# Down products of a two-layer MLP in seven block multiplications, with the activations' sums made where the up product stores its result

## The chip, the core and the metric

The kernel runs on one core of a Trainium2 chip. The core has a matrix engine (TensorE; in the profile PE for its matmuls and PEld for its weight loads), a vector engine (VectorE, DVE), a scalar engine (ScalarE, ACT), a general engine (GpSimd, POOL), and queues that start transfers between DRAM and the on-chip memory SBUF (all of this part's transfers are issued by SyncE, SP). Matmul results land in PSUM, which has eight banks of 2 KB per partition. The metric is the device time of one execution, in microseconds.

## The reference, cut to what matters

```python
def sq_relu_mlp(h, norm_w, w_up, w_down):
    return h + jnp.square(jax.nn.relu(rmsnorm(h, norm_w) @ w_up)) @ w_down
...
for layer in range(DEPTH):                 # DEPTH = 2
    if layer < N_A_LAYERS:                 # layer 0: Mamba-2 mixer
        ...
        hm = sq_relu_mlp(hm, mlp_norm_w[layer], w_up[layer], w_down[layer])
    else:                                  # layer 1: sliding-window attention
        ...
    hp = sq_relu_mlp(hp, mlp_norm_w[layer], w_up[layer], w_down[layer])
    hs = sq_relu_mlp(hs, mlp_norm_w[layer], w_up[layer], w_down[layer])
```

The model width is 1024, the MLP's inner width 4096. Layer 0 has 1104 tokens (1024 of the prompt, 64 of the samples, 16 meta tokens), layer 1 has 1088 (no meta tokens). All is fp32.

## The kernel before, in words

Activations lie with features on the 128 partitions and tokens along the free axis. The stream `h` has 8 feature tiles, the MLP's inner activations have 32, which the kernel takes as 16 pairs f = 0 to 15. Tokens go in three chunks of 384, 384 and 336 (layer 1: 320). An fp32 product is made of three reduced-precision ones (`mm3`, L174 to L179): weights and activations are both split into a high part `hi` and a remainder `lo`, and hi·hi, hi·lo and lo·hi are added up in PSUM. So every operand needs a copy to `hi` on ScalarE and a subtraction for `lo`: for weights on GpSimd (`wunit` L162 and L163, `wparts` L853 and L854), for stored activations on VectorE (`block_parts`, L950 and L951).

**Up product.** Pairs 0 and 1 are made by plain multiplication (`plain_up`), the other fourteen by `up_pair`, each as a 2 by 2 block product in seven multiplications in place of eight (a Strassen-like scheme). Its sums of stream blocks are made once, ahead, by `sides`, over pairs of token quarters (`PAIRS`); its sums of weight blocks are made per pair on VectorE (`up_weights`, L863 and L869), and its seven products go to four pairs of PSUM banks `ma` to `md` in the order of `CHAIN` (L757): a, d, c, b, a, c, d. A pair takes 7 x 24 = 168 matmuls of 276 columns (layer 1: 272). VectorE and ScalarE combine the products into the tile `r` (named `rx` in the profile; there is one such buffer), square the positive part, and three transfers (L918 to L920) store it to DRAM, in `rd[f]`. The first write of the next pair into `r` is ScalarE's copy of product 1 (L900).

**Down product.** Eight blocks b of two pairs each, `down_block`: the block's activations are loaded from `rd` (`block_load`, L945) while the block before is multiplied, and split (`block_parts`). A block has four weight units of 256 output columns, each two output tiles times three chunks times 12 matmuls, so 4 x 2 x 3 x 12 = 288 matmuls. Each PSUM result is added to the stream `hh` in SBUF by VectorE (L724). The last block goes with the norm that follows it (layer 0) or with the final norm (layer 1).

**What sets the order.** The program is written in one order, and a scheduler of the framework, which simulates the engines' times, lays each engine's instructions out anew; each engine and each queue then runs its list strictly in order. Tiles with `bufs=1` or 2 make a writer wait for the last reader of the buffer. In layer 1, `second_layer` writes the first plain pair, the sides of the first pair of quarters, the norm of token chunk 1, and the sides of the second pair of quarters in this order, because the quarters 0 and 3 of the first `PAIRS` entry need only the chunks 0 and 2.

The functions that the change touches, with the profile's line numbers:

Of the kernel before, what the change touches and what calls it, by code (L numbers as in the profile page):

```python
# [8 lines left out]
F32 = mybir.dt.float32  # L9
F32R = mybir.dt.float32r  # L10
# [6 lines left out]
P = 128  # L17
# [23 lines left out]
PAIRS = [(0, 3), (1, 2)]  # L41
# [98 lines left out]
class Kernel:  # L140
# [735 lines left out]
    def up_pair(self, layer, f, rd):  # L876
# [45 lines left out]
    def up(self, layer, rd, R0):  # L922

        with ExitStack() as cq:
# [4 lines left out]
            for f in range(2, 16):  # L929
                self.up_pair(layer, f, rd)  # L930
# [22 lines left out]
    def down_block(self, layer, rd, b, bufs, hts, chs, tail=0, done=None):  # L953

        if b < 7:
            self.block_load(rd, b + 1, bufs[b + 1])
        x = {c: tuple(bufs[b][:, e, :, o:o + n] for e in range(2)) for c, (o, n) in enumerate(chs)}
        self.down(self.i["w_down"][layer, b], 4, x, hts, chs, tail, done,
                  step=(lambda u: self.block_parts(u, bufs[b + 1])) if b < 7 else None)
# [481 lines left out]
    def halves(self, n):  # L1441

        return [self.S[:, e].rearrange("p (a b) n -> p a b n", a=2)[:, :, :, :n] for e in range(2)]

    def first_layer(self, cb):
        nc = self.nc
        rd = [self.dram.tile([P, 2, T], F32, name="r_d%d" % f) for f in range(16)]
        h_d = self.dram.tile([P, KT, T], F32, name="h_d")
        with ExitStack() as ch:
# [27 lines left out]
            with ExitStack() as ct:  # L1477
# [28 lines left out]

    def second_layer(self, nx, cb):
        nc = self.nc
        chs = [(0, 384), (384, 384), (768, 320)]
        rd = [self.dram.tile([P, 2, META], F32, name="r_e%d" % f) for f in range(16)]  # L1510
        h_d = self.dram.tile([P, KT, META], F32, name="h_e")
        qw = META // 4
        with ExitStack() as cx:
# [22 lines left out]
            with ExitStack() as ce:  # L1536
# [7 lines left out]
                for i in (1, 2, 3):  # L1544
                    step(i, 0)
# [3 lines left out]
                for i in (1, 2, 3):  # L1549
                    step(i, 1)  # L1550
# [8 lines left out]
            self.up(1, rd, R0)  # L1559
            cr.close()  # L1560
            self.banks(self.ctx, 3)
            self.more_banks(self.ctx, 4)
            big = self.pool("h2", right=True).tile([P, KT, META], F32, name="hh")
            hts = [big[:, :, o:o + n] for o, n in chs]
            self.load_stream(big, h_d)
            bufs = [R0] + self.halves(META) * 4
            self.down_block(1, rd, 0, bufs, hts, chs)
        self.acc = {}
        self.fpool = self.pool("fin")
        for b in range(1, 8):  # L1570
            self.down_block(1, rd, b, bufs, hts, chs, 2 if b == 7 else 0,
                            (lambda c, u: self.final(c, u, hts, chs)) if b == 7 else None)
# [53 lines left out]
def _lay(a):  # L1626
# [18 lines left out]
        "w_down": a["w_down"].reshape(2, 8, 4, P, 4, 256).transpose(0, 1, 4, 3, 2, 5),  # L1645
        "w_kv": a["w_kv"].reshape(KT, P, 4, P).transpose(2, 1, 0, 3),
# [42 lines left out]
```

## Time and profile before

| | before |
|---|---|
| median of 3 runs | 3054.63 us (3051.82 to 3058.26) |
| the profiled execution | 3061.61 us, span 3059.9 us |
| granted TensorE clock, mean | 0.982 |
| TensorE, matmuls | 2935.1 us busy (96%), 19174 matmuls |
| TensorE, weight loads | 2804.4 us (92%) |
| VectorE | 1723.2 us (56%) |
| ScalarE | 1368.0 us (45%) |
| GpSimd | 1234.6 us (40%) |
| DMA | 305.84 MB, mean 100 GB/s |

All times that the next sections quote are from the one profiled execution, which took 7.0 us more than the median. Line numbers with an L are those of the kernel before, if nothing else is said. A busy share is an average over stages with different limits: the two up products (layer 0 from about 1155 to 1456 us, layer 1 from about 2360 to 2657 us) and the two down products that follow them are the stages that the change touches, and they are read by themselves.

### The profile page before, as it was taken

To read this page: it belongs to the slowest core of one execution; us is meant where nothing else is said; L and a number is where in the kernel's file an instruction comes from. 1 tells how busy PE (TensorE), PEld (TensorE's weight loads), DVE (VectorE), ACT (ScalarE), POOL (GpSimd) and SP (SyncE) were. 2 spreads that over 40 slices of the span, in tenths; PEclk is the share of its full clock that TensorE was granted. 3 is DMA by queue.
4 is the path that set the end of the run, shared out by engine and by line. 5 is a ranking of instruction groups with operands and counts; after the bars stand their busy time and mean duration, and the time that the engine had idled before them with its cause. 6 is when DMAs were issued, how large, how long until landed. Compare 5 with 4: busy or idle time off the path is not lost.

```text
span 3059.9 us, 48866 instructions
## 1 busy us (share of the span) xinstructions
PE 2935.1 (96%) x19174; PEld 2804.4 (92%) x19174; DVE 1723.2 (56%) x2964; ACT 1368.0 (45%) x2578; POOL 1234.6 (40%) x1055
## 2 busy tenths in 40 slices
PE   6999999989999989999999999998988999999998
PEld 4988888878999989999999998887878999999998
DVE  5777777865565575333433356776788433333335
ACT  5455555545444555444211126555655445412113
POOL 4456666654233214444211235464642444312122
PEclk8999999999999999999999999998999999999999
DMA  3244444454122223333432212122223233512221
GB/s 123 75 116 114 118 123 116 118 139 143 57 71 76 83 74 121 110 115 120 178 108 72 71 42 67 60 90 87 93 98 110 97 104 114 198 55 101 105 71 66
DMA packets 189854, 305.84 MB, mean 100 GB/s; under 512 B 27624, under 2 KB 138088, under 8 KB 187560
## 3 DMA queue, kind: packets, MB, share of 16 engines
q1 hardware_dynamic: 189624, 302.72, 31.3%
q8 instruction: 150, 2.46, 0.3%
q14 instruction: 80, 0.66, 0.1%
HBM read 232.72 MB, written 70.92 MB: 99 GB/s over the span
## 4 chain that ended last, share of the span: by engine, by line
PE 52%; DVE 7%; ACT 3%; issue 2%; POOL 1%; DMA 0%; DVEq 0%; POOLq 0%; ACTq 0%
PE g L177 10%; PE g L178 10%; PE g L179 10%; PE md L179 2%; PE mc L179 2%; PE md L178 2%; PE mc L177 2%; PE mc L178 2%; PE md L177 2%; PE ma L179 2%; PE ma L177 2%; PE ma L178 2%; PE mb L179 1%; POOL w L163 1%; PE mb L178 1%
## 5 line engine op out<-in xcount | busy, mean ns | idle before, releaser
L177 PE MATMUL g<-S,w 128*128 128x384 f32 (+2 forms) x2904 | 971.9, 335 | 17.5 <-DVE hh L724 4.8
L178 PE MATMUL g<-S,w 128*128 128x384 f32 (+2 forms) x2904 | 974.4, 336 | 2.8 <-DVE S L317 2.2
L179 PE MATMUL g<-S,w 128*128 128x384 f32 (+2 forms) x2904 | 968.2, 334 | 1.8 <-POOL w L163 1.8
L163 POOL TENSOR_TENSOR w<-raw,w 128x1024 fp32r<-128x1024 f32 x188 | 463.6, 2468 | 983.2 <-ACT w L162 924.1
L177 PEld LDWEIGHTS g<-S,w 128*128 128x128 f32 x2904 | 549.7, 189 | 26.3 <-issue 5.8
L178 PEld LDWEIGHTS g<-S,w 128*128 128x128 f32 x2904 | 550.2, 189 | 10.0 <-DVE S L317 3.2
L179 PEld LDWEIGHTS g<-S,w 128*128 128x128 f32 x2904 | 550.7, 190 | 8.2 <-issue 3.6
L724 DVE TENSOR_TENSOR hh<-hh,g 128x384 f32<-128x384 f32 (+2 forms) x552 | 288.3, 533 | 440.7 <-PE g L179 439.9
L162 ACT CAST w<-raw 128x1024 fp32r<-128x1024 f32 x188 | 197.2, 1049 | 611.8 <-PE g L178 561.8
L854 POOL TENSOR_TENSOR w<-s,w 128x512 fp32r<-128x512 f32 x112 | 150.4, 1346 | 252.3 <-ACT w L853 251.4
L532 DVE SCALAR_TENSOR_TENSOR fm<-xp,cv,fm 128x1024 f32<-128x1024 f32 x96 | 164.7, 1716 | 31.0 <-ACT fm L513 30.4
L854 POOL TENSOR_TENSOR w<-raw,w 128x512 fp32r<-128x512 f32 x84 | 113.4, 1351 | 90.6 <-ACT w L853 56.6
L179 PE MATMUL ma<-S,w 128*128 128x276 f32 (+1 forms) x448 | 129.5, 289 | 0.0
L177 PE MATMUL ma<-S,w 128*128 128x276 f32 (+1 forms) x448 | 129.5, 289 | 0.0
L177 PE MATMUL g<-gh,w 128*128 128x384 f32 (+1 forms) x384 | 126.9, 332 | 2.5 <-DVE hh L724 1.2
L178 PE MATMUL ma<-S,w 128*128 128x276 f32 (+1 forms) x448 | 129.1, 288 | 0.0
L178 PE MATMUL g<-gl,w 128*128 128x384 f32 (+1 forms) x384 | 126.5, 330 | 0.0
L179 PE MATMUL g<-gh,w 128*128 128x384 f32 (+1 forms) x384 | 126.1, 329 | 0.0
L585 ACT ACTIVATE dec<-ab,acs 128x128 f32<-128x128 f32 (+1 forms) x288 | 91.1, 389 | 68.1 <-PE y L594 63.8
L863 DVE TENSOR_TENSOR s<-raw 128x512 f32<-128x512 f32 x56 | 45.8, 834 | 110.5 <-DMA raw<-in_w_up_dram 82.7
L630 POOL TENSOR_TENSOR yt<-yt,yo 128x256 f32<-128x256 f32 (+1 forms) x72 | 68.4, 949 | 88.4 <-DVE yt L627 82.4
L1143 ACT ACTIVATE es<-es,few 128x273 f32<-128x273 f32 (+2 forms) x136 | 70.9, 526 | 55.3 <-DVE few L1141 41.4
(390 smaller groups left out, 6715.2 us busy)
## 6 DMA issues: line engine op xcount, KB each, us to landing
raw<-in_w_up_dram SPq DMA_DIRECT2D x64, 512.0 KB
raw<-in_w_down_dram SPq DMA_DIRECT2D x64, 512.0 KB
raw<-in_w_in_dram SPq DMA_DIRECT2D x48, 512.0 KB
ab<-acs_d SPq DMA_DIRECT2D x64, 256.0 KB
S<-r_e SPq DMA_DIRECT2D x28, 544.0 KB
S<-r_d SPq DMA_DIRECT2D x24, 552.0 KB
raw<-in_w_q_dram SPq DMA_DIRECT2D x24, 512.0 KB
raw<-in_w_o_dram SPq DMA_DIRECT2D x24, 512.0 KB
```

The source lines that it names most:

```text
L162: nc.scalar.copy(out=wh, in_=raw)
L163: nc.gpsimd.tensor_tensor(out=wl, in0=raw, in1=wh.bitcast(F32), op=ALU.subtract)
L177: mm(out=out, lhsT=wh, rhs=xh, start=(first and k == 0), stop=False)
L178: mm(out=out, lhsT=wh, rhs=xl, start=False, stop=False)
L179: mm(out=out, lhsT=wl, rhs=xh, start=False, stop=(k == n - 1))
L532: nc.vector.scalar_tensor_tensor(out=acc[:, :SEQ], in0=xp[:, k:k + SEQ], scalar=cv[:, j, k:k + 1], in1=acc[:, :SEQ], op0=ALU.mult, op1=ALU ...
L585: nc.scalar.activation(out=dec[:n, h, :n], in_=ab[:n, h, :n], func=AF.Relu, scale=-1.0, bias=self.acs[:n, t, 4 * g + h:4 * g + h + 1])
L630: nc.gpsimd.tensor_tensor(out=yt[:, :, :no], in0=yt[:, :, :no], in1=yo[:, :, :no], op=ALU.add)
L724: nc.vector.tensor_tensor(out=hv, in0=hv, in1=pt[:, :n], op=ALU.add)
L854: nc.gpsimd.tensor_tensor(out=t[:, 1], in0=src, in1=t[:, 0].bitcast(F32), op=ALU.subtract)
L863: add = lambda a, b, op: (lambda t: (nc.vector.tensor_tensor(out=t, in0=a, in1=b, op=op), t)[1])(self.wsum([P] + sh))
L1143: nc.scalar.activation(out=e, in_=e, func=AF.Exp, bias=m[:, h:h + 1], accum_out=den[:, h:h + 1])
```

## The change

The middle twelve pairs, f = 2 to 13, get their down product in seven block multiplications too. They form four blocks of three pairs (`KB = 3`). The 2 by 2 blocks are: the two feature tiles of a pair, the output tiles p and p + 4, and the two token halves; so `PAIRS` becomes (0, 2), (1, 3), by which the two quarter pairs of the up product fill token halves.

- **Up.** `up_pair` of these twelve pairs adds five VectorE operations: three of 552 columns (`m1`, a new `r[:, 1]`, `u`) and two of 276 (`o5`). Each has both inputs in SBUF. Seven right sides are stored, in `rt`, by five transfers (`m1`, `r` with its four blocks, `u`, two pieces of `o5`). Pairs 14 and 15 store `r` to `rd` in one transfer, with no sums.
- **Down.** Block 0 (pairs 0 and 1) stays plain, now with all eight PSUM banks as single ones. While it runs, the first seven right sides, 128 partitions x 1656 elements (848 KB) each, are loaded and split. Then `down_blocks` goes through four blocks b, in each through four groups p of two output tiles. A group is seven products of 2 token pieces x 3 pairs x 3 = 18 matmuls of 276 columns (272 in layer 1), so 126 matmuls, into `ma` to `md` in the order of `CHAIN`. Per group VectorE makes four sums of weight blocks (384 columns; the weights are laid out for it as `w_downs`) and seven evictions of 552 columns, into `hh` or into a temporary `us` (the very first group's first one is ScalarE's); in block b = 3 it adds `us` to three parts of `hh` per group. GpSimd makes seven remainders of 384 columns per group.
- **The right sides' buffers.** Each block's seven slots are taken from `S`, `R0` and two new tiles `A5`, `A6`. Most of a block's slots are free only when the last group of the block before, or the first of its own, is under way, so five to seven splits per block (one ScalarE copy and one VectorE subtraction of 1656 elements each) stand around the change of blocks.
- **The last block** (pairs 14 and 15, b = 7) stays plain, as before.
- **Layer 1.** Both quarter pairs now need chunk 1, so the sides' steps 1 to 3 of the first quarter pair move behind `stream.norm(1)`.

Matmuls: six plain blocks of 288 become four blocks of 504, per layer 1728 become 2016, of 276 columns in place of 384, 384 and 336.

```diff
-PAIRS = [(0, 3), (1, 2)]
+PAIRS = [(0, 2), (1, 3)]
+KB = 3
...
-        rv = r.rearrange("p (f i) n -> p f i n", i=2)
-        nc.sync.dma_start(out=rd[f][:, :, 0:n], in_=rv[:, :, 0])
-        nc.sync.dma_start(out=rd[f][:, :, 3 * qw:4 * qw], in_=rv[:, :, 1, 0:qw])
-        nc.sync.dma_start(out=rd[f][:, :, n:3 * qw], in_=rv[:, :, 1, qw:n])
+        if not 2 <= f < 14:
+            nc.sync.dma_start(out=rd[f].rearrange("p f (i n) -> p (f i) n", i=2), in_=r)
+            return
+        sub = lambda out, x, y: nc.vector.tensor_tensor(out=out, in0=x, in1=y, op=ALU.subtract)
+        d = rt[(f - 2) // KB][:, :, :, (f - 2) % KB]
+        sub(m1, r[:, 1], r[:, 0])
+        nc.sync.dma_start(out=d[:, 0, 1], in_=m1)
+        sub(r[:, 1], r[:, 3], r[:, 1])
+        nc.sync.dma_start(out=d[:, :, 0], in_=r)
+        sub(u, r[:, 3], m1)
+        nc.sync.dma_start(out=d[:, 1, 1], in_=u)
+        for k in range(2):
+            t = self.n1("o5")[:, :qw]
+            cs = slice(k * qw, k * qw + qw)
+            sub(t, r[:, 2, cs], u[:, cs])
+            nc.sync.dma_start(out=d[:, 2, 1, cs], in_=t)
...
+    def down_weights(self, layer, b, p):
...
+        yield self.wparts(a11, sh)
+        s1 = add(a21, a22, ALU.add)
+        yield self.wparts(s1, sh)
+        d = add(a11, a21, ALU.subtract)
+        nc.vector.tensor_tensor(out=s1, in0=s1, in1=a11, op=ALU.subtract)
+        yield self.wparts(d, sh)
+        yield self.wparts(s1, sh)
+        yield self.wparts(a12, sh)
+        yield self.wparts(a22, sh)
+        yield self.wparts(add(a12, s1, ALU.subtract), sh)
...
+    def down_blocks(self, layer, rd, rt, R0, big, c0, chs):
...
+        slots = [A, B + A[:5], A[5:] + B + A[:3], A[3:] + A[:3]]
+        free = [(0, 1, 2, 3, 4), (0, 1, 2, 3, 4), (0, 1, 4, 5, 6), ()]
+        def load(b, i):
+            nc.sync.dma_start(out=slots[b][i][:, 1].bitcast(F32), in_=rt[b][:, i // 2, i % 2])
+        def parts(b, i):
+            x = slots[b][i]
+            nc.scalar.copy(out=x[:, 0], in_=x[:, 1].bitcast(F32))
+            nc.vector.tensor_tensor(out=x[:, 1], in0=x[:, 1].bitcast(F32), in1=x[:, 0].bitcast(F32), op=ALU.subtract)
...
+        def step(b, p, i):
+            if b == 3:
...
+            elif p == 0 and i == 0:
+                load(b + 1, 0)
+                load(b + 1, 1)
+            elif p in (1, 2) and i == 2:
+                parts(b + 1, p - 1)
+            elif p == 3 and i in free[b]:
+                load(b + 1, free[b].index(i) + 2)
+            if p == 3 and i > 4 and b < 3:
+                parts(b + 1, i - 3)
+            if p == 0 and i < 3 and b:
+                parts(b, 4 + i)
...
+        for b in range(4):
+            for p in range(4):
...
+                for i, (wh, wl) in enumerate(self.down_weights(layer, b, p)):
+                    e = self.CHAIN[i]
...
+                    x = slots[b][i]
+                    for k in range(2):
+                        cs = slice(k * qw, k * qw + qw)
+                        self.mm3(banks[e][:, 512 + (k - 1) * qw:512 + k * qw], [(wh[:, q], wl[:, q]) for q in range(KB)],
+                                 [(x[:, 0, q, cs], x[:, 1, q, cs]) for q in range(KB)], new)
+                    pv = banks[e][:, 512 - qw:512 + qw]
+                    to = (uv, hv[1][1], hv[1][1], uv, hv[0][0], hv[1][0], hv[0][1])[i]
+                    if i == 0 and b == 0:
+                        nc.scalar.copy(out=uv, in_=pv)
+                    else:
+                        tt(to, pv, to)
+                    if i == 3 and b == 3:
+                        for to in (hv[1][1], hv[1][0], hv[0][1]):
+                            tt(to, to, uv)
+                    step(b, p, i)
...
-                for i in (1, 2, 3):
-                    step(i, 0)
                 stream.norm(1)
                 for _ in plain:
                     pass
                 for i in (1, 2, 3):
-                    step(i, 1)
+                    for k in range(2):
+                        step(i, k)
```

The scheduler's lists show what moves. The first place is VectorE in the down product of layer 0. Before, inside a block (a block's activations are split while the one before is multiplied; `g` is a single PSUM bank):

```order
L724 TENSOR_TENSOR hh_14867<-hh_14867,g_15630 128x384
L951 TENSOR_TENSOR S_90<-S_90 128x1104
L724 TENSOR_TENSOR hh_14867<-hh_14867,g_15644 128x384
L951 TENSOR_TENSOR S_90<-S_90 128x1104 x2
L724 TENSOR_TENSOR hh_14867<-hh_14867,g_15658 128x336
L951 TENSOR_TENSOR S_90<-S_90 128x1104
L724 TENSOR_TENSOR hh_14867<-hh_14867,g_15672 128x384
```

Now, at the change from block b = 0 to b = 1 (L1056 is the eviction and L1024 the split, both lines of the kernel after; `md_15915` is the last product of the old block's last group, `ma_16067` the first of the new block):

```order
L1056 TENSOR_TENSOR hh_14966<-mc_15942,hh_14966 128x552
L1024 TENSOR_TENSOR S_90<-S_90 128x1656
L1056 TENSOR_TENSOR hh_14966<-md_15915,hh_14966 128x552
L1024 TENSOR_TENSOR S_90<-S_90 128x1656 x2
L1056 TENSOR_TENSOR us_14978<-ma_16067,us_14978 128x552
L1024 TENSOR_TENSOR A5_14979<-A5_14979 128x1656
L1056 TENSOR_TENSOR hh_14966<-md_16096,hh_14966 128x552
L1024 TENSOR_TENSOR A6_14980<-A6_14980 128x1656
L1056 TENSOR_TENSOR us_14978<-mb_16149,us_14978 128x552
L1056 TENSOR_TENSOR hh_14966<-mc_16124,hh_14966 128x552
```

Five splits, longer than before, now stand between the evictions that free the banks `md`, `ma` and `mc`, where before four stood in a block of 24 evictions. The second place is VectorE at the end of a pair in the up product of layer 0. Before (`n3_13166` is `u`, `s` are weight sums):

```order
L882 TENSOR_TENSOR rx_13040<-md_13080,n3_13166 128x552
L863 TENSOR_TENSOR s_13529<-raw_13497 128x512
L863 TENSOR_TENSOR s_13560<-raw_13495,raw_13497 128x512
L882 TENSOR_TENSOR rx_13269<-mc_13341,rx_13269 128x552
L869 TENSOR_TENSOR s_13529<-s_13529,raw_13495 128x512
```

Now (L885, L865 and L923 are lines of the kernel after):

```order
L885 TENSOR_TENSOR rx_13098<-md_13138,n3_13224 128x552
L865 TENSOR_TENSOR s_13605<-raw_13573 128x512
L923 TENSOR_TENSOR n3_13131<-rx_13098 128x552
L923 TENSOR_TENSOR rx_13098<-rx_13098 128x552
L923 TENSOR_TENSOR n3_13224<-rx_13098,n3_13131 128x552
L923 TENSOR_TENSOR o5_13326<-rx_13098,n3_13224 128x276
L923 TENSOR_TENSOR o5_13329<-rx_13098,n3_13224 128x276
L865 TENSOR_TENSOR s_13636<-raw_13571,raw_13573 128x512
L885 TENSOR_TENSOR rx_13336<-mc_13408,rx_13336 128x552
```

The five new operations stand between the last eviction of a pair and the first of the next that waits for the store of `r`, behind a weight sum that waits for its transfer. The order of TensorE's matmuls in the up product is the same as before.

More of the change, by code (lines that the diff above doesn't have):

```diff
@@ L929, in up @@
             for f in range(2, 16):
-                self.up_pair(layer, f, rd)
+                self.up_pair(layer, f, rd, rt)
                 if f == 8:
@@ L951, in block_parts, with down_block @@
         nc.vector.tensor_tensor(out=lo, in0=lo.bitcast(F32), in1=hi.bitcast(F32), op=ALU.subtract)
[L953 to L959, printed above, removed]
+    def down_block(self, layer, b, buf, hts, chs, tail=0, done=None, step=None):
+        x = {c: tuple(buf[:, e, :, o:o + n] for e in range(2)) for c, (o, n) in enumerate(chs)}
+        self.down(self.i["w_down"][layer, b], 4, x, hts, chs, tail, done, step=step)
@@ new lines, in down_weights, with add @@
+    def down_weights(self, layer, b, p):
+        nc = self.nc
+        sh = [KB, P]
+        raws = []
+        for j in range(2):
+            t = self.np.tile([P, 2, KB, P], F32, tag="n3", bufs=2, name="raw") if p % 2 else self.raw([P, 2, KB, P])
+            nc.sync.dma_start(out=t, in_=self.i["w_downs"][layer, b, p, :, j])
+            raws.append(t)
+        (a11, a12), (a21, a22) = ((t[:, 0], t[:, 1]) for t in raws)
+        def add(a, b, op):
+            t = self.np.tile([P] + sh, F32, tag="n1", bufs=5, name="s")
+            nc.vector.tensor_tensor(out=t, in0=a, in1=b, op=op)
+            return t
+        yield self.wparts(a11, sh)
[8 more added lines that the diff above has]
+        yield self.wparts(add(a12, s1, ALU.subtract), sh)
@@ L1447, in first_layer @@
         rd = [self.dram.tile([P, 2, T], F32, name="r_d%d" % f) for f in range(16)]
+        rt = [self.dram.tile([P, 4, 2, KB, T // 2], F32, name="t_d%d" % b) for b in range(4)]
         h_d = self.dram.tile([P, KT, T], F32, name="h_d")
@@ L1510, in second_layer @@
         rd = [self.dram.tile([P, 2, META], F32, name="r_e%d" % f) for f in range(16)]
+        rt = [self.dram.tile([P, 4, 2, KB, META // 2], F32, name="t_e%d" % b) for b in range(4)]
         h_d = self.dram.tile([P, KT, META], F32, name="h_e")
@@ L1558, in second_layer @@
             R0 = self.pool("R0", ctx=cx).tile([P, 2, 4, META], F32R, name="R0")
-            self.up(1, rd, R0)
+            self.up(1, rd, rt, R0)
             cr.close()
+            big = self.pool("h2", right=True).tile([P, KT, META], F32, name="hh")
+            self.load_stream(big, h_d)
+            with ExitStack() as c0:
+                self.down_blocks(1, rd, rt, R0, big, c0, chs)
             self.banks(self.ctx, 3)
             self.more_banks(self.ctx, 4)
-            big = self.pool("h2", right=True).tile([P, KT, META], F32, name="hh")
+            self.acc = {}
+            self.fpool = self.pool("fin", ctx=cx)
             hts = [big[:, :, o:o + n] for o, n in chs]
[L1565 to L1572, printed above, removed]
+            self.down_block(1, 7, R0, hts, chs, 2, lambda c, u: self.final(c, u, hts, chs))
     def mixer(self, c1):
```

57 lines of the change are left out of this document (46 added, 11 removed).

## The prediction, before the result was known

> **What bounds the kernel now.** I read the page's busy table first, then the table of stages for the four stages that the change touches:
>
> ```profile
> PE 2935.1 (96%) x19174; PEld 2804.4 (92%) x19174; DVE 1723.2 (56%) x2964; ACT 1368.0 (45%) x2578; POOL 1234.6 (40%) x1055
> ```
>
> ```profile
> core 0: us, PE busy (x) PEld busy (x) DVE busy (x) ACT busy (x) POOL busy (x), PEclk, DMA share, GB/s
> 1300.00:1350.00 50.00, 50.00 (x397) 50.00 (x396) 16.32 (x20) 26.10 (x43) 21.97 (x17) 1.00 0.32 104
> 1550.00:1600.00 50.00, 50.00 (x299) 50.00 (x299) 18.11 (x29) 9.75 (x9) 9.81 (x5) 1.00 0.28 97
> ...
> 2750.00:2800.00 50.00, 50.00 (x304) 50.00 (x303) 18.09 (x30) 8.63 (x8) 9.64 (x4) 1.00 0.25 88
> ```
>
> The first row lies in the up product of layer 0, the second and third in the down products of the two layers. In each PE is busy 50.00 us of 50 at the full granted clock and nothing else is near its limit. The view of PE's waits is empty from 1176.3 to 1442, from 1440 to 1800 and from 2400 to 2640 us. So a matmul saved there is time saved, until another engine falls behind.
>
> What a matmul costs, I take from the repeats of a stage in SyncE's list. Starts of one and the same transfer, one pair or one block apart (columns: start, duration):
>
> ```profile
> 1325.07 0.33 SPq L847 DMA_DIRECT2D raw<-in_w_up_dram  x1
> ...
> 1346.37 0.33 SPq L847 DMA_DIRECT2D raw<-in_w_up_dram  x1
> ...
> 1548.94 1.99 SPq L945 DMA_DIRECT2D S<-r_d  x4
> ...
> 1597.26 1.84 SPq L945 DMA_DIRECT2D S<-r_d  x4
> ```
>
> ```profile
> 2550.19 0.33 SPq L847 DMA_DIRECT2D raw<-in_w_up_dram  x1
> ...
> 2571.37 0.33 SPq L847 DMA_DIRECT2D raw<-in_w_up_dram  x1
> ...
> 2751.87 2.14 SPq L945 DMA_DIRECT2D S<-r_e  x4
> ...
> 2799.60 1.75 SPq L945 DMA_DIRECT2D S<-r_e  x4
> ```
>
> Layer 0: a pair takes 21.30 us for 168 matmuls, 126.8 ns each; a plain block 48.32 us for 288, 167.8 ns each. Layer 1: 21.18 us, 126.1 ns, and 47.73 us, 165.7 ns.
>
> **The change part by part.**
>
> *TensorE.* Six blocks go and 2016 matmuls come that have the up product's form: 276 (272) columns, fp32r, two pieces of a bank pair. Layer 0: 6 x 48.32 = 289.9 removed, 2016 x 126.8 ns = 255.6 added, -34.3. Layer 1: 286.4 removed, 254.2 added, -32.2. Together **-66.5 us**. This is the whole gain; the rest is what comes back.
>
> *VectorE and GpSimd in a group.* These rows price VectorE's operations with their partners:
>
> ```profile
> L882 DVE TENSOR_TENSOR rx<-rx,n x28: 726/1808/1822, 1175.2 to 2648.7; 128x552 f32<-128x552 f32 x14, 128x544 f32<-128x544 f32 x14
> L882 DVE TENSOR_TENSOR rx<-mc,n x28: 719/726/733, 1177.5 to 2654.0; 128x552 f32<-128x552 f32 x14, 128x544 f32<-128x544 f32 x14
> ...
> L951 DVE TENSOR_TENSOR S<-S x52: 1279/1294/1997, 1464.6 to 2952.2; 128x1088 fp32r<-128x1088 f32 x28, 128x1104 fp32r<-128x1104 f32 x24
> ```
>
> ```profile
> L863 DVE TENSOR_TENSOR s<-raw 128x512 f32<-128x512 f32 x24 | 19.2, 815 | 54.2 <-DMA raw<-in_w_up_dram 41.9 <-POOL w L854 12.4
> L882 DVE TENSOR_TENSOR rx<-rx,n 128x552 f32<-128x552 f32 x13 | 19.1, 1472 | 0.4
> L869 DVE TENSOR_TENSOR s<-s,raw 128x512 f32<-128x512 f32 x12 | 11.5, 961 | 14.3 <-POOL w L854 14.3
> ...
> L863 DVE TENSOR_TENSOR s<-raw,s 128x512 f32<-128x512 f32 x13 | 8.8, 681 | 0.0
> ...
> L854 POOL TENSOR_TENSOR w<-s,w x112: 1274/1292/2359, 1147.1 to 2640.1; 128x512 fp32r<-128x512 f32 x112
> ```
>
> (The forms with slashes are shortest, median, longest in ns over the whole run; those with bars are count, busy us and mean ns in the up product of layer 0.) A group of `down_blocks` is 126 x 126.8 ns = 15.98 us on PE. VectorE's seven evictions of 552 columns take 0.73 each (second row: one input from PSUM), its four weight sums 681 x 384/512 = 0.51 each, in all 7.2 us. GpSimd's remainders are 1292 x 384/512 = 0.97, seven make 6.8. An ordinary group is covered by PE twice over, and costs nothing.
>
> *The change of blocks.* A split of 1656 elements is 1294 x 1656/1096 = 1.96 us on VectorE, seven make 13.7, and most of them stand within two groups, the last of the old block and the first of the new. So these 31.9 us of PE carry 2 x 7.2 + 13.7 = 28.1 us of VectorE, at the last change (b = 2 to 3) 14.4 + 5 x 1.96 + four of block 7's splits at 1.29 + three `us` adds at 0.73 = 31.6. That is where cover runs out, for a reason that the first two rows show: the operation of 552 columns with both inputs in SBUF has a shortest time of 726 ns and a median of 1808, the one with an input from PSUM never passes 733. GpSimd's operations stretch likewise, from 1274 to 2359. The two engines get in each other's way when VectorE has two SBUF inputs, and a meeting costs VectorE some 1.08 us. Fifteen such operations stand at a change (seven splits, eight weight sums), with GpSimd busy 14 x 0.97 = 13.6 us of 31.9. None meeting: the lists are strictly in order, an eviction of `md` or `mc` waits behind a split or two, and PE loses perhaps 0.5 us. All meeting, at a mean overlap of three quarters of the 1.08: 15 x 0.81 = 12.2, so 28.1 + 12.2 = 40.3, 8.4 over. In the up product the 62 operations with two SBUF inputs stretch by 24 x 0.134 + 12 x 0.280 + 13 x 0.746 = 16.3 us over 681 (for 552 columns, 726), 0.26 each. I take this row mean: 15 x 0.26 = 3.9, so 32.0 against 31.9 at the first two changes and 35.5, 3.6 over, at the last. With an eviction's wait behind the splits I take 2.5, 2.5 and 4, **+9 per layer, +18** in all, with ends of +3 (6 x 0.5) and +50 (6 x 8.4).
>
> The Trainium skill ("SBUF — State Buffer", section "SBUF: two separate sides") says that VectorE and GpSimd share a port pair under an exclusive lock held for a whole instruction, so that a VectorE operation with two SBUF inputs and a GpSimd operation that reads SBUF block each other fully. The trace agrees (726 against 1808 ns). By that rule taken at its word, each of the fifteen operations would meet one, and the sum would use the upper end, +50 in place of +18.
>
> *The other parts of the down product.* The `us` adds of b = 3 (three a group, both inputs in SBUF) stand among evictions, +1 per layer, +2; ends 0 and +8. The first seven right sides are loaded during block 0, with the stream and the weights some 13.7 MB. The highest rate a row shows:
>
> ```profile
> 1448.00:1450.00 2.00, 2.00 (x18) 2.00 (x18) 0.00 (x0) 1.06 (x2) 1.75 (x1) 1.00 1.05 426
> ```
>
> At about 400 GB/s that is 34 of 48.3 us, hidden by block 0's matmuls; at half the rate it would be 20 us late per layer. I take +0.5 each, **+3 with the `us` adds**.
>
> *The up product's store.* Five VectorE operations (726 to 1808 ns) and two more transfers per pair; VectorE has the room (16.32 of 50 us). What matters is the loop through the single buffer `r`:
>
> ```profile
> 1333.96 0.62 ACT L900 COPY rx<-md 128x552 f32<-128x552 f32 x1 [0.80 <-DMA r_d<-rx]
> ...
> 1335.21 0.73 DVE L882 TENSOR_TENSOR rx<-mc,rx 128x552 f32<-128x552 f32 x1 [2.90 <-PE mc L179]
> ...
> ACT rx L900 <- DMA r_d<-rx: 27.8, 12, 6.1
> ```
>
> ```profile
> 1326.05 0.73 DVE L882 TENSOR_TENSOR rx<-md,n 128x552 f32<-128x552 f32 x1 [2.32 <-PE md L179]
> ...
> 1329.36 0.69 DVE L863 TENSOR_TENSOR s<-raw 128x512 f32<-128x512 f32 x1 [2.58 <-DMA raw<-in_w_up_dram]
> ```
>
> `md` of the last product is evicted at 1326.05; ScalarE's copy of product 1 into `r` goes at 1333.96, having waited 0.80 us for the store, in the early pairs up to 6.1 us. What it feeds is the eviction of `mc` at 1335.21, which must be done when PE's product 5 writes `mc`: five products of 3.04 us (21.30/7) after 1326.0, at 1341.2. From 1333.96 that leaves 1341.2 - 1333.96 - 0.62 - 0.73 - 0.15 (semaphores) = 5.7 us. After, `r` leaves only when the first two differences are made, behind a weight sum that itself waits for its transfer (1329.36), and with three quarters more bytes (seven blocks in place of four). I estimate its landing 2.7 to 4.3 us later than now (two differences of 0.73 to 1.81, the wait of up to 2.58, the longer transfer, less what they overlap), so 5.7 - 4.3 = 1.4 us or more is left in the steady pairs, and nothing in the first ones, where the wait is already 6.1. **+3 us** over both layers, ends 0 and +12.
>
> *Layer 1's start.* Around it PE waits:
>
> ```profile
> PE g L223 <- ACT msh L221: 6.7, 1, 6.7
> PE md L177 <- ACT w L853: 2.7, 1, 2.7
> ...
> 2299.92 1.27 DVE L795 TENSOR_TENSOR t<-X 128x1088 f32<-128x1088 f32 x1
> ...
> 2314.31 0.55 DVE L222 TENSOR_TENSOR msl<-acc,msh 128x384 fp32r<-128x384 f32 x1
> ```
>
> The 6.7 us are PE's wait for the norm of chunk 1, whose `msl` stands on VectorE behind the first quarter pair's sides (L795). The sides move behind it, so most of this wait goes; the sides then come late to the first pairs, which can lengthen the 2.7 us. **-2.5**, ends -6.7 and +3.
>
> Sum: -66.5 + 18 + 3 + 3 - 2.5 = -45.0. Against the profiled execution's 3061.6 that is 3016.6; this execution stood 7.0 above the median, so on the scale of the median **3009.6 us**.
>
> **The rivals.**
>
> *B, nothing comes back.* GpSimd and VectorE miss each other and the splits fit. For it: 28.1 of 31.9 us without a meeting, and the scheduler fills a wait for `md` with half a product into `mc`. Then -66.5 + 3 - 2.5, about **2989**.
>
> *C, VectorE and GpSimd lock each other at every change of blocks.* For it: the median of 1808, not 726, in the one operation whose place is fixed relative to GpSimd's. Against it: the splits' own median of 1294 beside its minimum of 1279, though GpSimd is less busy there (9.81 of 50 us). Then -66.5 + 50 + 3.5, **3042**.
>
> *D, slower: the store loop lengthens each pair.* The copy of product 1 waits for `r`, its dependent eviction frees `mc` late, and PE stands in each of the 24 changed pairs. It decides from a landing 5.7 + 1.9 = 7.6 us later than now: at 1.9 us a pair (45/24) no gain is left. At 3 us a pair it costs 72, **3082**. For it: the 6.1 us waits, and the larger store on five transfers; against it: the DMA share of 0.32 in this stage.
>
> *E, a wait at each group takes the gain.* The last product's `md` is needed again after one product of the next group, now 18 matmuls (2.3 us) in place of 24 (3.04 us in the up product, where the view of waits is empty). The eviction's 0.73 us and its semaphores fit, unless VectorE's list is behind. At 2 us in each of the 32 groups, 64 us, nothing is left: **3052**. This is also how the change could fail to do what it says.
>
> **How the numbers follow.** Forecast 0.58 (its own range 2990 to 3033), B 0.14, C 0.14, E 0.06, D 0.08. A measurement of this kernel can tell about 0.2%, 6 us, from no change. Faster by more: forecast, B and C, less a little of C's upper end: 0.85. Within: E and that little, 0.07. Slower: D, 0.08. The range takes in B below and C above with some of C's spread: 2983 to 3046.
>
> **What the changed profile would show.** Right: about 19,750 matmuls (19174 + 2 x 288); a pair still 21.3 us apart; the splits at a block's change between 1.96 and 3 us; PE's waits on evictions from VectorE there, 2 to 4 us per change, and hardly any elsewhere in the down product; the 6.7 us wait gone. Wrong: PE's waits between pairs of the up product, with `r`'s store as their end (D); waits in every group (E); block changes of over 8 us (C); or a spacing in `down_blocks` other than 126.8 ns, which would resize the main term.

## The result, and the profile after

| | before | after |
|---|---|---|
| median | 3054.24 us (4 runs, 3051.82 to 3058.26) | 3009.99 us (4 runs, 3003.57 to 3013.72) |
| ratio | | 0.9852 (95% interval 0.9828 to 0.9875) |
| the profiled execution | 3061.61 us, span 3059.9 | 3013.72 us, span 3012.0 |

The change made the kernel 44 us faster. The profiled execution of after is the slowest of its four, 3.7 us above their median. The busy row of its page:

```profile
PE 2876.1 (95%) x19750; PEld 2743.4 (91%) x19750; DVE 1963.2 (65%) x3172; ACT 1453.5 (48%) x2770; POOL 1397.4 (46%) x1231
```

There are 576 matmuls more and TensorE is busy 59 us less. To see where the time went I cut both profiles at matmuls that both programs have: the first into `ma` (start of the up product's pairs) and the first of blocks 0 and 7 into a single bank `g`. The views by tile give first and last starts (of all forms; `g<-R` are the blocks that read `R0`). Before, layer 0, block 0 and block 7:

```profile
L177 PE MATMUL g<-R,w x33: 312/334/342, 1453.6 to 1469.9; 128*128 128x384 f32 x24, 128*128 128x336 f32 x9
...
L177 PE MATMUL g<-R,w x96: 312/334/341, 1791.9 to 1839.8; 128*128 128x384 f32 x64, 128*128 128x336 f32 x32
```

After, the same two, and those of layer 1:

```profile
L179 PE MATMUL g<-R,w x96: 312/334/341, 1451.9 to 1499.8; 128*128 128x384 f32 x64, 128*128 128x336 f32 x32
L179 PE MATMUL g<-R,w x96: 312/334/411, 1770.4 to 1818.4; 128*128 128x384 f32 x64, 128*128 128x336 f32 x32
...
L179 PE MATMUL g<-R,w x96: 306/334/338, 2630.3 to 2677.3; 128*128 128x384 f32 x64, 128*128 128x320 f32 x32
...
L179 PE MATMUL g<-R,w x96: 303/334/422, 2943.9 to 2993.0; 128*128 128x384 f32 x64, 128*128 128x320 f32 x32
```

| stretch | before | after | difference | forecast |
|---|---|---|---|---|
| start to the first `ma`, layer 0 | 1155.2 | 1151.7 | -3.5 | 0 |
| up product, layer 0 | 298.4 | 300.2 | +1.8 | +3 with layer 1 |
| block 0 to block 7, layer 0 | 338.3 | 318.5 | -19.8 | -23.8 |
| block 7 to the first `ma`, layer 1 | 558.9 | 554.2 | -4.7 | -2.5 |
| up product, layer 1 | 307.0 | 305.7 | -1.3 | |
| block 0 to block 7, layer 1 | 334.1 | 313.6 | -20.5 | -21.7 |
| block 7 to the end | 68.0 | 68.1 | +0.1 | 0 |

(Before, the layer 1 blocks are taken as seven periods of 47.73 us.) Most of the gain, 40.3 of 47.9 us, lies in the two down products. Within them, the view of TensorE's waits from 1500 to 1770 us, empty before, now has four rows:

```profile
PE md L179 <- DVE hh L1056: 3.7, 2, 2.3
PE ma L179 <- DVE us L1056: 3.2, 2, 1.6
PE mc L179 <- DVE hh L1056: 1.3, 2, 0.6
PE mb L181 <- POOL w L856: 0.3, 1, 0.3
```

VectorE's timeline shows where they are. The change from b = 0 to b = 1 (columns: start, duration, what it is, and in brackets the idle time before it):

```profile
1538.30 0.73 DVE L1056 TENSOR_TENSOR hh<-md,hh 128x552 f32<-128x552 f32 x1 [4.98 <-PE md L181]
...
1554.31 0.73 DVE L1056 TENSOR_TENSOR hh<-md,hh 128x552 f32<-128x552 f32 x1 [4.98 <-PE md L181]
...
1567.82 2.06 DVE L1024 TENSOR_TENSOR S<-S 128x1656 fp32r<-128x1656 f32 x1
1569.80 0.72 DVE L1056 TENSOR_TENSOR hh<-md,hh 128x552 f32<-128x552 f32 x1
1570.44 4.68 DVE L1024 TENSOR_TENSOR S<-S 128x1656 fp32r<-128x1656 f32 x2
1575.04 0.72 DVE L1056 TENSOR_TENSOR us<-ma,us 128x552 f32<-128x552 f32 x1
1575.69 2.03 DVE L1024 TENSOR_TENSOR A<-A 128x1656 fp32r<-128x1656 f32 x1
1577.64 0.72 DVE L1056 TENSOR_TENSOR hh<-md,hh 128x552 f32<-128x552 f32 x1
...
1605.96 0.73 DVE L1056 TENSOR_TENSOR hh<-md,hh 128x552 f32<-128x552 f32 x1 [2.70 <-PE md L181]
```

In an ordinary group VectorE stands idle for 4.98 us before `md` comes, and groups follow each other in 16.0 us (1538.30 to 1554.31). Between 1562.3 and 1588.1 no row has a bracket: VectorE never waits, and evictions come one or two splits after their matmuls. The next `md` that VectorE waits for, at the same place in its group, comes 51.65 us and three groups later, 3.6 more than three groups take. In the same way the other changes cost 3.4 and 5.6 us in layer 0, and 2.1, 2.2 and 7.6 in layer 1.

At the last change of each layer a part of this is the clock, which the rows of waits don't show. Right after TensorE's longest wait there (2.30 us for `md` in layer 0, 2.69 in layer 1) the granted clock reads 0.50 for 3.41 us, and matmuls that start 127 ns apart elsewhere start 230 ns apart. Three stretches of equal length, the halved one of layer 0, one 10 us later, and the halved one of layer 1 (clock in the third column from the end, the first count in brackets is TensorE's matmuls):

```profile
1709.42:1712.83 3.41, 3.41 (x17) 3.41 (x17) 3.41 (x3) 0.00 (x0) 2.23 (x1) 0.50 0.00 0
1719.42:1722.83 3.41, 3.41 (x29) 3.41 (x29) 3.41 (x7) 0.85 (x2) 1.46 (x2) 1.00 0.08 10
2890.43:2893.84 3.41, 3.41 (x17) 3.41 (x16) 3.41 (x7) 0.51 (x1) 1.62 (x2) 0.50 0.00 0
```

I estimate this at 3.41 x (1 - 127/230) = 1.5 us of the 5.6 and of the 7.6.

The up product kept its pace, one pair in 21.33 us (SyncE's list):

```profile
1260.28 2.36 SPq L849 DMA_DIRECT2D raw<-in_w_up_dram  x2
...
1281.61 2.35 SPq L849 DMA_DIRECT2D raw<-in_w_up_dram  x2
```

### The profile page after: what moved, and what is told of

Read it like the earlier page. It is cut to its first block, busy times and chain, and to the rows that moved or that the text cites. A ratio compares the mean times of both kernels' runs of the same rounds, so it can differ in the third digit from the quotient of the medians.

```text
span 3012.0 us, 50781 instructions
## 1 busy us (share of the span) xinstructions
PE 2876.1 (95%) x19750; PEld 2743.4 (91%) x19750; DVE 1963.2 (65%) x3172; ACT 1453.5 (48%) x2770; POOL 1397.4 (46%) x1231
## 4 chain that ended last, share of the span: by engine, by line
PE 45%; DVE 9%; ACT 4%; issue 3%; POOL 2%; DMA 2%; SPq 0%; DVEq 0%; POOLq 0%; ACTq 0%
PE g L179 3%; PE g L180 3%; PE g L181 3%; PE mc L179 3%; PE mc L181 3%; PE mc L180 3%; PE md L181 3%; PE md L180 3%; PE md L179 3%; PE ma L179 3%; PE ma L181 3%; PE ma L180 3%; PE mb L179 1%; PE mb L180 1%; PE mb L181 1%
## 5 line engine op out<-in xcount | busy, mean ns | idle before, releaser
L179 PE MATMUL g<-S,w 128*128 128x384 f32 (+3 forms) x1656 | 561.3, 339 | 17.5 <-DVE hh L726 4.8
L180 PE MATMUL g<-S,w 128*128 128x384 f32 (+3 forms) x1656 | 562.8, 340 | 3.6 <-DVE S L319 3.0
L181 PE MATMUL g<-S,w 128*128 128x384 f32 (+3 forms) x1656 | 557.5, 337 | 1.8 <-POOL w L165 1.8
L856 POOL TENSOR_TENSOR w<-s,w 128x384 fp32r<-128x384 f32 (+1 forms) x240 | 326.5, 1363 | 367.0 <-ACT w L855 355.2
L856 POOL TENSOR_TENSOR w<-raw,w 128x384 fp32r<-128x384 f32 (+1 forms) x180 | 222.8, 1240 | 268.0 <-ACT w L855 251.9
L179 PEld LDWEIGHTS g<-S,w 128*128 128x128 f32 (+1 forms) x1656 | 315.1, 190 | 26.2 <-issue 5.9
L180 PEld LDWEIGHTS g<-S,w 128*128 128x128 f32 (+1 forms) x1656 | 315.1, 190 | 10.6 <-DVE S L319 4.1
L181 PEld LDWEIGHTS g<-S,w 128*128 128x128 f32 (+1 forms) x1656 | 315.2, 190 | 8.0 <-issue 3.3
L855 ACT CAST w<-s 128x384 fp32r<-128x384 f32 (+1 forms) x240 | 134.4, 562 | 211.3 <-PE ma L181 69.9
L179 PE MATMUL ma<-S,w 128*128 128x276 f32 (+1 forms) x736 | 212.9, 289 | 5.0 <-DVE us L1056 5.0
L180 PE MATMUL ma<-S,w 128*128 128x276 f32 (+1 forms) x736 | 212.5, 289 | 1.1 <-DVE S L820 0.9
L181 PE MATMUL ma<-S,w 128*128 128x276 f32 (+1 forms) x736 | 212.4, 289 | 0.0
L726 DVE TENSOR_TENSOR hh<-hh,g 128x384 f32<-128x384 f32 (+2 forms) x264 | 134.1, 530 | 68.8 <-PE g L181 68.3
L179 PE MATMUL md<-S,w 128*128 128x276 f32 (+1 forms) x464 | 135.5, 292 | 8.9 <-DVE hh L1056 8.7
L179 PEld LDWEIGHTS ma<-S,w 128*128 128x128 f32 x736 | 138.6, 188 | 5.7 <-ACT w L855 3.6
L180 PEld LDWEIGHTS ma<-S,w 128*128 128x128 f32 x736 | 138.7, 188 | 1.6 <-DVE S L820 1.1
L181 PEld LDWEIGHTS ma<-S,w 128*128 128x128 f32 x736 | 138.5, 188 | 0.0
L179 PE MATMUL mc<-S,w 128*128 128x276 f32 (+1 forms) x464 | 134.7, 290 | 3.9 <-DVE hh L1056 2.6
```

What stands on the lines that cost most here:

```text
L179: mm(out=out, lhsT=wh, rhs=xh, start=(first and k == 0), stop=False)
L180: mm(out=out, lhsT=wh, rhs=xl, start=False, stop=False)
L181: mm(out=out, lhsT=wl, rhs=xh, start=False, stop=(k == n - 1))
L726: nc.vector.tensor_tensor(out=hv, in0=hv, in1=pt[:, :n], op=ALU.add)
L855: nc.scalar.copy(out=t[:, 0], in_=src)
L856: nc.gpsimd.tensor_tensor(out=t[:, 1], in0=src, in1=t[:, 0].bitcast(F32), op=ALU.subtract)
```

## The experiments

**What costs at a change of blocks.** My theory was that VectorE's own work there, in its strict order and stretched by GpSimd, is longer than TensorE's. The rivals: the loads of the right sides come too late, or the length of the list alone counts. Four runs pull these apart.

*e1*, the VectorE half of the splits left out for b = 1 to 3 (the remainder slot keeps the unsplit value):

```diff
             nc.scalar.copy(out=x[:, 0], in_=x[:, 1].bitcast(F32))
-            nc.vector.tensor_tensor(out=x[:, 1], in0=x[:, 1].bitcast(F32), in1=x[:, 0].bitcast(F32), op=ALU.subtract)
+            if b == 0:
+                nc.vector.tensor_tensor(out=x[:, 1], in0=x[:, 1].bitcast(F32), in1=x[:, 0].bitcast(F32), op=ALU.subtract)
```

> Left out: VectorE's half of the split (x - hi) of the right sides of blocks b = 1 to 3 in both layers, 42 operations of 1.88 to 2.7 us; the remainder slot keeps the unsplit value. ScalarE's copy, all loads, evictions, sums and matmuls stay. My theory (at a change of blocks VectorE's strictly ordered list is longer than PE's work, so PE waits behind it): the changes, which now cost 3.6 + 3.4 + 5.6 us in layer 0 and about 2.2 + 2.3 + 5 in layer 1, lose nearly all of it: 3010 goes to about 2990. Rival (the loads of the right sides come too late, since their slots are freed late): the loads stay where they are, 3010 stays within 5 us.

Measured: 2986.26 us, ratio to before 0.9768 (0.9749 to 0.9788). In layer 0, block 7 starts 312.7 us after the up product's last matmul into `ma` (324.7 after: the changes' 12.6 us are gone), and the view of TensorE's waits has one row there:

```profile
PE md L179 <- DVE hh L1057: 0.3, 1, 0.3
```

All loads are still in place, so they are not what TensorE waits for.

*e2*, GpSimd's remainders of the weights left out in the down blocks (the matmuls take the high part twice):

```diff
-        yield self.wparts(a11, sh)
+        yield self.whigh(a11, sh)      # t[:, 0], t[:, 0]: no GpSimd operation
...
```

> Left out: GpSimd's remainders of the weights in the seven-product down blocks (7 per group, 224 in all); the matmuls that used them take the high part instead, so their count stays. My theory: VectorE's operations with two SBUF inputs no longer meet GpSimd, so at a change the seven splits fall from about 14.6 to 13.2 us and the weight sums from 8 to 4.3, 5 us less than PE's cover needs: the 12.6 us of layer 0's changes fall to about 3, in all 3010 to about 2994. Rival (the list's length alone counts, meetings don't): within 4 us of 3010.

Measured: 2993.19 us, ratio 0.9790 (0.9772 to 0.9807). All VectorE operations are still there, but they are shorter. The costliest groups of VectorE in layer 0's blocks, after (columns: count, busy us, mean ns, idle time before):

```profile
L1024 DVE TENSOR_TENSOR S<-S 128x1656 fp32r<-128x1656 f32 x13 | 27.2, 2108 | 2.0 <-ACT S L1023 2.0
L986 DVE TENSOR_TENSOR s<-raw 128x384 f32<-128x384 f32 x28 | 24.9, 928 | 0.0
```

and in e2:

```profile
L1029 DVE TENSOR_TENSOR S<-S 128x1656 fp32r<-128x1656 f32 x13 | 24.1, 1877 | 1.5 <-ACT S L1028 1.5
...
L991 DVE TENSOR_TENSOR s<-raw 128x384 f32<-128x384 f32 x28 | 14.3, 553 | 0.0
```

The same 28 weight sums take 24.9 us beside GpSimd and 14.3 without it. Without meetings the unchanged list fits under TensorE's time (one wait of 1.2 us is left). So the list's length alone doesn't make the loss.

*e5*, one VectorE operation more at each change (a split slot's maximum with itself):

```diff
                 parts(b, 4 + i)
+                if i == 1:
+                    x = slots[b][5][:, 1]
+                    nc.vector.tensor_tensor(out=x, in0=x.bitcast(F32), in1=x.bitcast(F32), op=ALU.max)
```

> The changed kernel with one more VectorE operation at each change of blocks (the maximum of a split slot with itself, 1656 elements, 128 partitions, some 1.9 to 2.3 us; the values stay). My theory (VectorE's time is the bound at a change): each extra microsecond there is a microsecond of the whole, six times 1.9 to 2.3: 3010 becomes 3021 to 3024. Rival (PE waits there for something else, and VectorE has slack): within 4 us of 3010.

Measured: 3026.42 us, ratio 0.9906 (0.9890 to 0.9923), 16.5 us more than the changed kernel by the ratios, for six operations of 1.94 us (11.7 us); its profile also has a third stretch of 3.4 us at half the clock, another 1.5 us by the estimate above. VectorE has no slack at a change.

*e6*, the seventh split of blocks 1 to 3 moved to GpSimd:

```diff
-                parts(b, 4 + i)
+                parts(b, 4 + i, nc.gpsimd if i == 2 else None)
```

> The changed kernel with the last of the seven splits of blocks 1 to 3 made by GpSimd (about 1656 x 1.01/384 = 4.4 us) in place of VectorE (1.9 to 2.1 us). My theory (both engines' time with two SBUF inputs adds up at a change, 17.5 + 14.1 us in 32 now, 15.6 + 18.5 then): no gain, 3010 to 3018. Rival (only VectorE's own list is too long): 1.9 us less at each of six changes, 2999.

Measured: 3019.55 us, ratio 0.9879 (0.9864 to 0.9894): slower than the changed kernel by 8 us, with intervals that just overlap, though VectorE has an operation less at each change; the rival's gain of 11 us is ruled out. The rows of GpSimd and of VectorE in layer 0's blocks:

```profile
L1024 POOL TENSOR_TENSOR S<-S 128x1656 fp32r<-128x1656 f32 x3 | 14.1, 4716 | 1.8 <-ACT S L1023 1.8
```

```profile
L1024 DVE TENSOR_TENSOR S<-S 128x1656 fp32r<-128x1656 f32 x10 | 28.6, 2859 | 1.5 <-ACT S L1023 1.5
```

The three operations gone cost VectorE more than they took: ten splits now take 28.6 us, where thirteen took 27.2. TensorE's own waits for GpSimd stay at 0.3 us in layer 0's blocks, as in the changed kernel, so it isn't GpSimd that is late. Here, moving an operation with two SBUF inputs from VectorE to GpSimd did not get the work done sooner: beside the longer GpSimd operation VectorE's splits took longer.

**The up product.** *e3*, the five differences left out, the transfers kept:

```diff
-        sub(m1, r[:, 1], r[:, 0])
-        nc.sync.dma_start(out=d[:, 0, 1], in_=m1)
+        nc.sync.dma_start(out=d[:, 0, 1], in_=r[:, 1])
...
```

> Left out: the five VectorE differences per pair in the up product's store, 24 pairs; the five transfers stay with the same bytes, taken from r directly. My theory: the up product has room on VectorE and the store loop slack, so the sums cost nothing: 3010 within 4 us, the span from the first to the last matmul into ma in layer 0 at 292 to 294 us. Rival (the differences delay the store of r and PE with it): 1 us per pair or more, 24 us or more faster.

Measured: 3014.96 us, ratio 0.9863 (0.9847 to 0.9880), not to be told from the changed kernel's 0.9852. In the profiles, from the first to the last `ma` of layer 0, e3 takes 292.3 us, as forecast, and the changed kernel 294.0; in layer 1, 299.3 and 299.5. So the differences cost 1.7 us in the one up product and next to nothing in the other. TensorE's waits of the changed kernel from 1157 to 1450 us have one row, `mc` on `rx`, of 1.4 us; e3 has none.

The loop through `r` came as near as forecast. In a steady pair of the changed kernel ScalarE's copy of product 1 and the eviction of `mc` behind it are

```profile
1314.65 0.62 ACT L903 COPY rx<-md 128x552 f32<-128x552 f32 x1 [1.70 <-DMA t_d<-rx]
1315.30 0.73 DVE L885 TENSOR_TENSOR rx<-mc,rx 128x552 f32<-128x552 f32 x1 [3.37 <-ACT rx L903]
```

The last `md` was evicted at 1302.89, so the copy starts 11.8 us after it; before (1326.05, 1333.96) it was 7.9. That is 3.9 us later, within the estimate of 2.7 to 4.3. The eviction, which waited for TensorE before, now waits for this copy; it ends at 1316.03, 1.9 us before product 5 writes `mc` (1317.91).

**Layer 1's order.** *e4*, the kernel before with the new `PAIRS`, the moved sides and one store per pair:

> The kernel before with the new pairs of token quarters, the sides of layer 1 moved behind the norm of chunk 1, and one store per up pair; down product as before. My theory: this move alone takes PE's 6.7 us wait for that norm away and is worth 3 to 6 us: 3054 to about 3050. Rival (the wait only moves to the first pairs of the up product): 3054 within 2 us. The first matmul into ma in layer 0 at 1155 or 1152 us also tells whether the 3.5 us that the changed kernel was earlier there come from the change.

Measured: 3051.26 us (10 runs), ratio 0.9987 (0.9976 to 0.9998): 4 us faster, with an interval of 0.6 to 7.3, for the three edits together. The 6.7 us wait (`PE g L223 <- ACT msh L221`) is gone in e4 and after; the wait for the first pair's weights has grown from 2.7 to 3.7 in both, and two of 0.9 each stand beside it, of which before had one, of 0.2 (the rows of after):

```profile
PE md L179 <- ACT w L855: 3.7, 1, 3.7
PE ma L180 <- DVE S L820: 0.9, 1, 0.9
PE md L181 <- POOL w L856: 0.9, 1, 0.9
```

The first `ma` of layer 0 starts at 1152.8 us in e4, which has nothing of the down product's change, and between 1151.1 and 1155.4 in all runs. The 3.5 us at the start of the table are no part of the change.

**Can the loss be had back?** *e7*, the last block's four splits held back (in the changed kernel all four stand at the change from b = 2 to b = 3):

```diff
                 if p > 0 and i == 2:
-                    self.block_parts(p - 1, R0)
+                    with self.tc.issue_after(self.last_cast):
+                        self.block_parts(p - 1, R0)
...
```

> The changed kernel with the four splits of the last plain block (pairs 14 and 15; 1.3 to 1.8 us each on VectorE) held back behind the weight copies of the groups in which the program writes them, in place of all four at the change from b = 2 to b = 3. My theory: the last change has 5.8 us less on VectorE, its loss (5.6 us in layer 0) falls to that of the other two (3.5) or below, 2 to 5 us per layer, 3010 to about 3003. Rival (the splits there fill gaps and cost nothing): within 3 us of 3010.

Measured: 3001.27 us, ratio 0.9820 (0.9806 to 0.9835). By the ratios that is 9.8 us less than the changed kernel, with intervals that just touch. Its profile has 3.7 us less from the last `ma` to block 7 in layer 0 and 3.8 in layer 1; together 7.5 of the median's 8.7 us. Some 3 us of this, by the estimate above, is the clock: in e7 it isn't halved at the last changes. Between them its profile has another 8.8 us less in the attention stage, which I don't count: there the granted clock of one and the same stretch of the program differs from run to run, as below.

*e9*, on top of e7, one of the seven right sides is split in the up product:

```diff
             sub(t, r[:, 2, cs], u[:, cs])
+            th = self.np.tile([P, 384], F32R, tag="n1", bufs=5, name="o5h")[:, :qw]
+            nc.scalar.copy(out=th, in_=t)
+            sub(t, t, th.bitcast(F32))
             nc.sync.dma_start(out=d[:, 2, 1, cs], in_=t)
+            nc.sync.dma_start(out=rt[4 + (f - 2) // KB][:, (f - 2) % KB, cs], in_=th.bitcast(F32))
```

> As e7 (last block's splits held back), and the sixth right side (i = 5, made in two pieces in the up product's store) is split there, where VectorE has room: two more ScalarE copies, two VectorE differences and two transfers per pair; the down product loads its two halves and splits only six of seven. My theory: 1.9 us of VectorE and what it meets leave each of the six changes; e5 showed 16.4 us for adding 1.9 to 2.3 at each, so 9 to 15 us less than e7's 3001: 2986 to 2992. Rival (with e7 the changes fit, or the up product's store loop now stalls): 3001 or more.

Measured: 2998.58 us, ratio 0.9814 (0.9796 to 0.9831), not to be told from e7. My forecast was 9 to 15 us; in the profile the two down stages gained 2.7 and 4.0 us (block 7 of layer 0 starts 318.3 us after the last `ma` in place of 321.0). Not all of the loss was gone with e7: measured from e1's 312.7, 8.3 us of it were left in layer 0. One operation less at each change brought 2.7 of these, where one more had cost 7.0 there in e5, the price that I had used.

*e10*, a second right side split there as well:

> As e9, with the fourth right side (i = 3, u) split in the up product too; 5 of 7 splits are left in the down product. The floor is e7 without any loss at changes, about 2980 by e1 (which leaves all splits out and reaches 2986 with the last block's splits in the way). My theory: a further gain of 0 to 8 us over e9, 2980 to 2990, until the changes fit under PE's time. Rival (six small tiles in a ring of five make ScalarE wait in the up product, and PE behind it): slower than e9, by 1 us a pair 24.

Measured: 3006.82 us, ratio 0.9838 (0.9819 to 0.9856), 8 us slower than e9 by the medians, with intervals that overlap. The down stage of layer 0 gains another 4.5 us (313.8), but the first to the last `ma` of its up product takes 299.9 in place of 294.2 us. TensorE's waits there:

```profile
PE mc L179 <- DVE rx L885: 4.1, 5, 1.6
PE ma L179 <- ACT n L901: 0.7, 1, 0.7
```

The rival came about in a smaller size, 5.7 us in layer 0 and 1.5 in layer 1 (302.1 in place of 300.6): the eviction of `mc` is late in some pairs. Why it is late, whether by the ring of five tiles or by VectorE's longer list, the run doesn't tell.

*e8*, blocks of two pairs (`KB = 2`, six blocks), whose smaller slots leave room to load a whole block ahead:

```diff
-KB = 3
+KB = 2
...
+        slots = [A[:7], B, A[:7], B, A[:7], A[7:] + B[4:] + A[:3]]
```

> Six blocks of two pairs in place of four of three (KB = 2): slots are two thirds as large, fifteen fit in the same memory, so that all seven of the next block are free a whole block ahead, up to the last block. VectorE makes 168 evictions per layer in place of 112, the split bytes are the same. In this version the scheduler still puts the splits of a block as early as their slots come free. My theory: a group is 84 matmuls, 10.65 us on PE, and VectorE's mean is 5.1 + 1.5 + 2.2 = 8.8, with meetings 10; gathered splits make it wait at places: 2995 to 3015. Rival (what counts is only how many splits stand at a change where they are urgent): down by the 23 us that the changes now lose, about 2990.

Measured: 3047.26 us (10 runs), ratio 0.9978 (0.9967 to 0.9989): nearly all of the gain is lost, and my range was far too low.

*e11*, the same with the splits held back behind the weight copy of their group, one or two to a group; three of the last of these blocks stay as they were, and the last plain block's four are held back as in e7:

```diff
                 if (p, i) != (0, 2) and i in (2, 5):
-                    parts(b + 1, 2 * p - (i == 2))
+                    with self.tc.issue_after(self.last_cast):
+                        parts(b + 1, 2 * p - (i == 2))
```

> e8 (blocks of two pairs, 3047) with each split held back behind the weight copy of the group in which the program writes it, so that the splits stand one or two to a group in place of gathered. My theory: e8 lost by gathered splits and by VectorE's density (5.1 us of evictions in a group of 10.65 on PE); spread, the mean of 8.8 to 10 fits, 3000 to 3025. Rival (the density alone and the short products, 1.5 us each, lose it): 3040 or more.

Measured: 2996.57 us, ratio 0.9796 (0.9770 to 0.9823), 51 us less than e8 with the same operations; it is faster than the kernel before and the changed one (0.9852, 0.9828 to 0.9875), and not to be told from e7. What part of the 51 us the last plain block's splits make, as in e7, the run doesn't separate. Two stretches of the blocks in e8 (columns as in the prediction's table of stages):

```profile
1600.00:1650.00 50.00, 45.00 (x338) 44.32 (x337) 35.85 (x50) 17.23 (x35) 24.87 (x29) 0.97 0.37 122
1650.00:1700.00 50.00, 46.90 (x352) 46.06 (x351) 37.66 (x54) 16.91 (x35) 26.83 (x29) 0.97 0.34 121
```

and in e11:

```profile
1600.00:1650.00 50.00, 50.00 (x396) 50.00 (x395) 43.74 (x61) 21.97 (x42) 26.60 (x34) 1.00 0.41 133
1650.00:1700.00 50.00, 50.00 (x396) 50.00 (x395) 43.91 (x60) 20.15 (x40) 26.86 (x33) 1.00 0.38 133
```

In e11 VectorE is busy 88% of the time and TensorE doesn't stop; in e8 VectorE is busy 72 to 75%, TensorE stands idle for 6 to 10%, and with a clock of 0.97 it gets through 338 and 352 matmuls where e11 does 396. So how busy VectorE is on average doesn't decide; the order of its list does. Of e8's waits of TensorE from 1500 to 1786 us, 9.6 us are on evictions, and 8.0 on weight parts from ScalarE and GpSimd; whether those are late for the same reason isn't shown. My price for density (3000 to 3025) was too high.

## Why the prediction was right, and where it was not

The forecast was 3009.6 us, the median is 3009.99. By its steps:

- **The main term (-66.5)** holds in its rate: a group takes 16.0 us in layer 0, forecast 15.98, so 126 matmuls of 276 columns cost what the up product's spacing said.
- **The changes of blocks (+18)** are the right mechanism, shown by e1, e2 and e5 with e6 in line, and too small in size: 3.6, 3.4 and 5.6 us in layer 0 (forecast 2.5, 2.5, 4), 2.1, 2.2 and 7.6 in layer 1, in all 24.5. Of the 6.5 us that are missing, about 3 are the halved clock at the two last changes, which the prediction does not have at all. The step that was mis-sized is the stretch by GpSimd, in two ways. I had taken 0.26 us for each operation, the mean of the up product; in layer 0's blocks the weight sums took 0.93 in place of 0.55 and the splits into `S` 2.11 in place of 1.88 (e2), which makes 4.6 us for eight sums and seven splits in place of 3.9. And at the last change I counted the same fifteen operations, though the list priced there has twenty with two SBUF inputs (five splits, four of block 7's, eight sums, three `us` adds). How much each of the two makes can't be split: without the clock the first two changes of layer 1 came out below the forecast, the others at it or above. At five of the six changes the price of rival C, 8.4 each, was far off; the last one of layer 1 came near it, with 1.5 us of its 7.6 from the clock. The lock that the Trainium skill states ("SBUF — State Buffer", section "SBUF: two separate sides") is what e2 and e6 look like: a GpSimd operation of 4.7 us lengthens VectorE's splits from 2.11 to 2.86. But not every operation meets one, and the sum by the rule at its word, +50, came out twice too high.
- **Block 0, the `us` adds (+3):** block 0 took 48.4 us as before (1451.9 to 1500.3), so the loads were hidden. The adds can't be told apart from the changes.
- **The up product's store (+3):** +0.5 by the table, 1.7 and 0.2 in the two layers by e3's profile, too little for its median to show.
- **Layer 1's start (-2.5):** -4 (-7.3 to -0.6) by e4. The -4.7 of the table can't show it: this stretch took between 545.4 and 559.4 us in the profiles of the changed kernels. The wait of 6.7 us went and 1.0 to 2.6 came back in the first pair.
- The terms that came out better (-2.2 and -2.5) and 3.5 us at the start that are run to run made up for 5.2 us that the down products kept back. The sum is nearer than its parts: that the median lies 0.4 us from the forecast is luck, and what is earned is the main term, the place of the loss and its cause.

The rivals: B (nothing comes back, 2989) is what e1 and e2 look like, not the changed kernel. D, the store loop, keeps 1.9 us in a steady pair, where the prediction had left 1.4 or more; e10 shows it bite when more is put in. E needed 2 us in each group; after, ordinary groups have no wait. In e8, where a product is 12 matmuls, waits did take the gain, but e11 has the same short products without them.

## What to carry to other kernels

When matmuls are saved, look for the stretch where another engine's strictly ordered list is longer than what is left of TensorE's time, and add up that stretch by itself; a share of 65% for the whole kernel said nothing about 26 us at 100%. Before adding work or buffers there, spread it: held-back splits won about 9 us in e7 and 51 between e8 and e11, with no operation saved. And price a VectorE operation with two SBUF inputs with GpSimd's work beside it, since moving such work to GpSimd made it worse.

## What the runs showed of the hardware that was not expected

- Whether two operations meet depends on the phase of the program. The operation of 552 columns with both inputs in SBUF, median 1808 ns before, has a median of 732 after, in the same place of the same product; of the new differences the first ones at times stretch to 1820, most don't:

```profile
L885 DVE TENSOR_TENSOR rx<-rx,n x28: 712/732/1821, 1171.8 to 2622.2; 128x552 f32<-128x552 f32 x14, 128x544 f32<-128x544 f32 x14
L923 DVE TENSOR_TENSOR n<-rx x24: 710/720/1820, 1181.1 to 2593.7; 128x552 f32<-128x552 f32 x12, 128x544 f32<-128x544 f32 x12
```

- A wait of TensorE can be followed by a stretch at half the clock, so that it costs more than it lasts. After, this came behind the waits of 2.30 and 2.69 us at the last changes (the rows are above). The mean clock of the four seven-product blocks reads 0.99 or less in after, e3, e5, e6 and e8, where TensorE waits most, and 1.00 in e1, e2, e7, e9, e10 and e11. What makes the clock fall, and from how long a wait on, isn't shown.

- The granted clock in the attention stage of layer 1, which all these kernels share but for its order, differs between profiles. The stretch of 70 us that starts 280 us after block 7's first matmul (clock in the third column from the end), after:

```profile
2050.40:2120.40 70.00, 64.43 (x464) 54.07 (x464) 45.79 (x144) 42.18 (x117) 29.34 (x25) 0.87 0.30 94
```

and in e7:

```profile
2047.60:2117.60 70.00, 66.30 (x515) 55.84 (x513) 47.26 (x155) 42.74 (x125) 27.80 (x26) 0.95 0.29 89
```

  From block 7 to the first `ma` of layer 1 the profiles took 545.4 (e7) to 559.4 us (e10), so one profiled execution can't price an edit of a few microseconds in that stretch; medians over runs and the cut by stages did. Whether the order or the clock makes the difference stays open.
